# One recursion step of Strassen-Winograd: high and low matmuls in two series, and two weight sums made by accumulating transfers

## The chip, the core and the metric

The kernel runs on one core of a Trainium2 chip. A core has five engines with queues of their own: TensorE (PE; its weight loads are listed as PEld), VectorE (DVE), ScalarE (ACT), GpSimd (POOL) and SyncE (SP). SP, ACT and POOL also issue DMA transfers. The metric is the device time of one execution in microseconds (us), lower is better.

## The reference

One residual layer over 512 tokens of width 2048:

```
u = RMSNorm(h); [q|k|v|conv_a|conv_b|gate_attn|gate_conv] = u @ W_in
m = sigmoid(gate_attn) * y_attn + sigmoid(gate_conv) * y_conv
h = h + RMSNorm(m @ W_out)
h = h + RMSNorm((silu(u2 @ W_gate) * (u2 @ W_up)) @ W_down),   u2 = RMSNorm(h)
```

y_attn is a neighbourhood attention of 8 heads on an 8 x 64 grid with a learned bias, y_conv a gated depthwise convolution of width 31 with a layer norm. D_FF is 5632. All is float32.

## The kernel before, in words

Activations lie transposed: 16 tiles of 128 features by 512 tokens. Float32 products are made from rounded halves: x = high + low, and a product is high x high + high x low + low x high, three matmuls. A plain product (`gemm`) streams 512 columns per matmul and takes the weights in chunks of 512 KB: SP loads a chunk, ACT casts its high half (L124), DVE subtracts to get the low half (L125).

**The sigmoid gates and most of the feed-forward's first product go through `strassen` (L205).** One call makes two column blocks of 128 outputs for all 512 tokens. Its matrices are cut in two ways each: the inner dimension into features 0 to 1023 and 1024 to 2047, the tokens into halves A and B, and the outputs into two blocks, w0 and w1. So A11 and A12 are the halves of w0, A21 and A22 those of w1, and in Winograd's form seven products of quarter size do the work of eight:

```
S1 = A21 + A22, S2 = S1 - A11, S3 = A11 - A21, S4 = A12 - S2
T1 = B12 - B11, T2 = B22 - T1, T3 = B22 - B12, T4 = B21 - T2
A11 B11, A12 B21, S1 T1, S2 T2, S3 T3, S4 B22, A22 T4
```

(T4 and the place of A22 are such that the block of w1 comes out as p5 and y below.) The sums T are made once per stage by `winograd_t` (L190) and kept in SBUF, in slots whose first 256 columns are the high half and whose last 256 are the low half. The sums S are made in every call. `product` (L230) casts the weights' high half on ACT (L232), makes the low half on DVE (L234), and then, for each of 8 feature tiles, issues a matmul of the high weights with all 512 columns (L237: high and low activations at once) and one of the low weights with the first 256 columns (L238).

S1 is loaded by SP as A21 (L249), and GpSimd adds A22 to it in a transfer that accumulates (L250). S2, S3 and S4 are DVE sums (L222, L222, L266). A11, A21, A22 and A12 come by SP (`quarter`, L217), into six buffers that the stages of `gemm` use too. Three PSUM banks x, y and z take the products; ACT copies some out (`copied` L227, `done` L244), DVE adds (L257, L262, L264), and `joined` (L273) adds the two column halves of a result. There are 14 calls for the gates (L564, names g2 to g15) and 39 for the feed-forward (L740, names f5 to f43); between the two lie the rest of the mixer and the feed-forward's start.

**What sets the order.** The program is written in the order of the mathematics; a scheduler orders each engine's instructions by priority and by what is free, and places the buffers. A load is issued as soon as a buffer of its kind is free, and each DMA queue works in order. Only instructions handed to `keep_in_program_order` keep the order as written (some loads and the sums of squares). Activations, normalised inputs, T sums, results and squares share one pool `sp` of 66 slots of 2 KB per partition (L68). S1 has a kind of buffer of its own with two buffers of 4 KB ("S1"), the other sums another with two ("S"); at the end of the kernel loads of the residual use them as well (L798).

Of the kernel before, what the change touches and what calls it, by code (L numbers as in the profile page):

```python
# [25 lines left out]
F32 = mybir.dt.float32  # L26
F32R = mybir.dt.float32r
AF = mybir.ActivationFunctionType
ALU = mybir.AluOpType
AX = mybir.AxisListType  # L30

P = 128
# [30 lines left out]
def hybrid_block(ctx: ExitStack, tc, xT, vecs, rpb, mask, w_c0, w_qk, w_v, w_gg, w_cg, w_ao, w_co, w_out, w_g0, w_gu, w_dn, outT):  # L63
    nc = tc.nc
    PSUM = bass.MemoryType.PSUM
    const = ctx.enter_context(tc.tile_pool(name="const", bufs=1))
    wp = ctx.enter_context(tc.tile_pool(name="wp", bufs=3))
    sp = ctx.enter_context(tc.tile_pool(name="sp", bufs=66))  # L68
    sm_ctx = ExitStack()
    mm = ctx.enter_context(tc.tile_pool(name="mm", bufs=4, space=PSUM))  # L70
    at = ctx.enter_context(tc.tile_pool(name="at", bufs=4, space=PSUM))
# [4 lines left out]
    HT, HN = KT // 2, NT // 2  # L76
    A, B = slice(0, HN), slice(HN, NT)
# [4 lines left out]
    def bank(name):  # L82
        return mm.tile([P, NT], F32, tag="mm", name=name)
# [32 lines left out]
    def wchunk(src, name, parts=1):  # L116
        w = src.shape[-1]
        raw = wp.tile([P, 1024], F32, tag="raw", name=f"raw_{name}", bufs=6)[:, :w]
        hi = wp.tile([P, 1024], F32R, tag="whi", name=f"whi_{name}")[:, :w]
        lo = wp.tile([P, 1024], F32R, tag="wlo", name=f"wlo_{name}")[:, :w]  # L120
        for n in range(parts):
            s = slice(n * w // parts, (n + 1) * w // parts)
            nc.sync.dma_start(raw[:, s], src[:, s])
            nc.scalar.copy(hi[:, s], raw[:, s])  # L124
            nc.vector.tensor_tensor(out=lo[:, s], in0=raw[:, s], in1=hi[:, s].bitcast(F32), op=ALU.subtract)  # L125
        taps(rate)
        return hi, lo
# [61 lines left out]

    def winograd_t(u1, u2, t12, t34):  # L190

        nc.vector.tensor_tensor(out=t12[:, A], in0=u1[:, B], in1=u1[:, A], op=ALU.subtract)
        nc.vector.tensor_tensor(out=t12[:, B], in0=u2[:, B], in1=t12[:, A], op=ALU.subtract)
        nc.vector.tensor_tensor(out=t34[:, A], in0=u2[:, B], in1=u1[:, B], op=ALU.subtract)
        nc.vector.tensor_tensor(out=t34[:, B], in0=u2[:, A], in1=t12[:, B], op=ALU.subtract)

    def operands(b11, b2, t12, t34):
        return {
            "11": b11,
            **{n: [t[i] for t in b2] for i, n in enumerate(("21", "22"))},  # L200
            **{n: [t[i] for t in t12] for i, n in enumerate(("T1", "T2"))},
            **{n: [t[i] for t in t34] for i, n in enumerate(("T3", "T4"))},
        }

    def strassen(w0, w1, op, name, n):  # L205

        x, y, z = ((bank, abank)[n % 2](f"{name}_{i}") for i in range(3))

        def quarter(w, c):
            raw = wp.tile([P, 1024], F32, tag="raw", name=f"{name}q", bufs=6)
            nc.sync.dma_start(raw, w[:, c * 1024 : (c + 1) * 1024])  # L217
            return raw

        def wsum(a, b, op, i):  # L220
            t = stp.tile([P, 1024], F32, tag="S", name=f"{name}s{i}")
            nc.vector.tensor_tensor(out=t, in0=a, in1=b, op=op)  # L222
            return t

        def copied(ps, i):
            t = stp.tile([P, NT], F32, tag="quad", name=f"{name}v{i}", bufs=3)
            nc.scalar.copy(t, ps)  # L227
            return t

        def product(ps, w, b, first=False, last=False):  # L230
            hi = wp.tile([P, 1024], F32R, tag="whi", name=f"{name}h")
            nc.scalar.copy(hi, w)  # L232
            lo = wp.tile([P, 1024], F32R, tag="wlo", name=f"{name}l")
            nc.vector.tensor_tensor(out=lo, in0=w, in1=hi.bitcast(F32), op=ALU.subtract)  # L234
            for k, t in enumerate(op[b]):
                s = slice(k * P, (k + 1) * P)
                nc.tensor.matmul(ps, hi[:, s], t, start=first and k == 0, stop=False, skip_group_check=True)  # L237
                nc.tensor.matmul(  # L238
                    ps[:, A], lo[:, s], t[:, A], start=False, stop=last and k == HT - 1, skip_group_check=True
                )  # L240

        def done(ps, i):
            t = stp.tile([P, HN], F32, tag="half", name=f"{name}c{i}", bufs=2)
            nc.scalar.copy(t, ps[:, B])  # L244
            return ps[:, A], t


        s1 = stp.tile([P, 1024], F32, tag="S1", name=f"{name}s1")
        nc.sync.dma_start(s1, w1[:, :1024])  # L249
        nc.gpsimd.dma_start(s1, w1[:, 1024:], accum_op=ALU.add)  # L250
        a11, a21, a22, a12 = quarter(w0, 0), quarter(w1, 0), quarter(w1, 1), quarter(w0, 1)
        product(x, a11, "11", first=True)
        s2 = wsum(s1, a11, ALU.subtract, 2)
        p1 = copied(x, 1)
        product(y, s2, "T2", first=True)
        product(z, s1, "T1", first=True)
        nc.vector.tensor_tensor(out=y, in0=y, in1=p1, op=ALU.add)  # L257
        u2 = copied(y, 2)
        s3 = wsum(a11, a21, ALU.subtract, 3)
        product(y, s3, "T3")  # L260
        p5 = copied(z, 3)
        nc.vector.tensor_tensor(out=z, in0=z, in1=u2, op=ALU.add)  # L262
        product(x, a12, "21", last=True)
        nc.vector.tensor_tensor(out=p5, in0=y, in1=p5, op=ALU.add)  # L264
        s4 = s2
        nc.vector.tensor_tensor(out=s4, in0=a12, in1=s2, op=ALU.subtract)  # L266
        c11 = done(x, 1)
        product(z, s4, "22", last=True)
        c12 = done(z, 2)
        product(y, a22, "T4", last=True)  # L270
        return c11, c12, done(y, 3), (p5[:, A], p5[:, B])
# [117 lines left out]
    for c in range(HT):  # L389
# [3 lines left out]
        hi, lo = wchunk(w_c0[c], f"c0_{c}", 1 if c else 2)  # L393
# [33 lines left out]
    for half in range(2):  # L427
        rate = R_V[half]
        pv = [(bank, abank)[half](f"pv{half}_{t}") for t in range(NB)]
        for c in range(HT):  # L430
            if len(u) < 2 * c + 2:
                normalize(c)
            hi, lo = wchunk(w_v[half, :, c * 1024 : (c + 1) * 1024], f"v{half}_{c}")
            for k in range(2):
                s = slice(k * NT, (k + 1) * NT)
# [72 lines left out]
    for h in range(H):  # L508
        bm = bias_of(h)
        qk = []  # L510
        for i in range(2):
            ps = bank(f"qk{h}_{i}")
# [7 lines left out]
    stp = ctx.enter_context(tc.tile_pool(name="stp", bufs=2))  # L520
# [3 lines left out]
    b11, b2, t12, t34 = [], [], [], []  # L524
    pg = [bank(f"g0_{n}") for n in range(4)]
    for c in range(HT):
        hi, lo = wchunk(w_gg[c], f"g0_{c}")
        un = stp.tile([P, 2, NT], F32, tag="S", name=f"un{c}")
        for j, k in enumerate((c, c + HT)):
            ah, al = u[k]  # L530
            for n, ps in enumerate(pg):
                s = slice((j * 4 + n) * P, (j * 4 + n + 1) * P)
# [4 lines left out]
                out=un[:, j], in0=ah.bitcast(F32), in1=al.bitcast(F32), op=ALU.add  # L537
# [24 lines left out]
    op = operands(b11, b2, t12, t34)  # L562
    for i in range(2, KT):
        c11, c12, c21, c22 = strassen(w_cg[2 * CT + i], w_cg[2 * CT + KT + i], op, f"g{i}", i)  # L564
        if i == KT - 1:
            ya = [load_ya(h) for h in range(YA_EARLY)]
        ga, gb = slot(f"ga{i}"), slot(f"gb{i}")
        joined(ga[:, A], c11)
        joined(ga[:, B], c12)
        nc.scalar.activation(ga, ga, AF.Sigmoid)  # L570
        nc.scalar.dma_start(g_d[i], ga)
        joined(gb[:, B], c22)
        joined(gb[:, A], c21)
        nc.scalar.activation(gb, gb, AF.Sigmoid)
        nc.scalar.dma_start(g_d[KT + i], gb)


# [54 lines left out]
    f, acc = [], None  # L632
    for i in range(KT - 2):
        ps = bank(f"po{i}")
# [55 lines left out]
    for j in range(3):  # L690
        t = stp.tile([P, 2, NT], F32, tag="S", name=f"sg{j}")
        t, up = t[:, 0], t[:, 1]
# [10 lines left out]
    for c in range(HT):  # L703
        hi, lo = wchunk(w_g0[1, c], f"f1_{c}")
        for k in range(2):
            i = 2 * c + k
# [7 lines left out]
            for n in range(4):  # L714
                s = slice((k * 4 + n) * P, (k * 4 + n + 1) * P)
                for m, cols in enumerate((A, B)):
                    plain(pf[n][:, cols], hi[:, s], lo[:, s], moving[m], i + m == 0, i == KT - 1)
            if i >= HT:
                t12, t34 = slot(f"t12_{i}"), slot(f"t34_{i}")
# [3 lines left out]
    for j in range(2):  # L723
        t = slot(f"sg{3 + j}")
# [5 lines left out]
    op = operands(b11, b2, b_t12, b_t34)  # L730
# [6 lines left out]
    for j in range(5, FT):  # L737
        if j == FT - EARLY_AT:
            acts = [load(k) for k in range(EARLY)]
        c11, c12, c21, c22 = strassen(w_gu[j], w_gu[FT + j], op, f"f{j}", j)  # L740
        if j == FT - 1:
            acts += [load(k) for k in range(EARLY, EARLY + MORE)]
        t, up = slot(f"sg{j}"), slot(f"su{j}")
        joined(t[:, A], c11)
        joined(t[:, B], c12)
        nc.scalar.activation(t, t, AF.Silu)  # L746
        joined(up[:, B], c22)
        joined(up[:, A], c21)
        nc.vector.tensor_tensor(out=t, in0=t, in1=up, op=ALU.mult)
        nc.scalar.dma_start(a_d[j], t)  # L750


# [2 lines left out]
    for half in range(2):  # L755
        for g in range(KT // 2):
            last = half == 0 and g == KT // 2 - 1
# [37 lines left out]

    ha = []
    for i in range(0, KT - 4, 4):
        t = stp.tile([P, 4, HN], F32, tag="S" if i else "S1", name=f"ha{i}")  # L798
        nc.gpsimd.dma_start(t, h_d[i : i + 4, :, A].rearrange("k p t -> p k t"))
        ha += [t[:, m] for m in range(4)]  # L800
    for i in range(KT - 4, KT, 2):
        t = stp.tile([P, 2, HN], F32, tag="quad", name=f"ha{i}", bufs=3)
# [3 lines left out]
    s1, s2 = halves(r4, acc + sq, "r4", 0, pin=True)  # L806
# [107 lines left out]
```

## Time and profile before

| | us |
|---|---|
| median of 3 runs | 2596.47 (2594.53 to 2597.9) |
| the profiled execution's own time | 2599.95 |
| its span, first to last instruction | 2597.8 |
| TensorE busy | 2547.3 (98%) |
| VectorE busy | 1744.4 (67%) |
| ScalarE busy | 1074.8 (41%) |
| GpSimd busy | 264.7 (10%) |

The mean granted TensorE clock is 0.993 of full speed. 385.42 MB move by DMA, 148 GB/s over the span. Stages by the trace, from the span's start: convolution inputs, V and attention to 480 us; the sums T for the gates to 547; the gates' calls to 825; the output products of attention and convolution to 1005; W_out to 1190; the feed-forward's first chunk to 1263 and its sums T to 1312; its calls to 2085; the down projection to 2580; the last norm and the stores to 2598.

How to read it: the profile is one execution. Matmuls overlap, so the distance between the starts of two of them says what one costs, and not its own duration. In a timeline a row has its start in us, its duration in us, engine, line, operation, what it writes and reads, and behind it in brackets how long the engine had stood idle and what ended that.

### The profile page before, as it was taken

To read this page: it belongs to the slowest core of one execution; us is meant where nothing else is said; L and a number is where in the kernel's file an instruction comes from. 1 tells how busy PE (TensorE), PEld (TensorE's weight loads), DVE (VectorE), ACT (ScalarE), POOL (GpSimd) and SP (SyncE) were. 2 spreads that over 40 slices of the span, in tenths; PEclk is the share of its full clock that TensorE was granted. 3 is DMA by queue.
4 is the path that set the end of the run, shared out by engine and by line. 5 is a ranking of instruction groups with operands and counts; after the bars stand their busy time and mean duration, and the time that the engine had idled before them with its cause. 6 is when DMAs were issued, how large, how long until landed. Compare 5 with 4: busy or idle time off the path is not lost.

```text
span 2597.8 us, 33528 instructions
## 1 busy us (share of the span) xinstructions
PE 2547.3 (98%) x13078; PEld 2165.4 (83%) x13078; DVE 1744.4 (67%) x2224; ACT 1074.8 (41%) x1560; POOL 264.7 (10%) x290
## 2 busy tenths in 40 slices
PE   9999999999999999998999999999999999999996
PEld 8888888778888888887988888888888878888886
DVE  5999895677776654339887777777777842233336
ACT  5223333455555422224555555555555532233222
POOL 0110222320000021004100000000000110010003
PEclk9999999999999999999999999999999999999998
DMA  6244323356667445234356556555655653353334
GB/s 214 93 128 148 109 94 107 101 157 184 181 189 249 139 138 183 97 106 146 110 161 181 167 167 180 175 170 167 186 167 167 196 185 97 97 170 100 95 93 139
DMA packets 124623, 385.42 MB, mean 148 GB/s; under 512 B 14256, under 2 KB 21552, under 8 KB 124464
## 3 DMA queue, kind: packets, MB, share of 16 engines
q1 hardware_dynamic: 96464, 311.47, 36.8%
q0 software_dynamic: 13024, 45.62, 8.5%
q10 hardware_dynamic: 14976, 26.19, 2.7%
q8 instruction: 102, 1.67, 0.3%
q14 instruction: 57, 0.47, 0.1%
HBM read 350.72 MB, written 32.51 MB: 148 GB/s over the span
## 4 chain that ended last, share of the span: by engine, by line
PE 93%; DVE 4%; issue 1%; DMA 1%; ACT 1%; POOL 1%; POOLq 0%; DVEq 0%; ACTq 0%; SPq 0%
PE f L237 20%; PE f L238 10%; PE g L237 7%; PE pd L170 5%; PE pd L173 5%; PE pd L174 5%; PE g L238 4%; PE po L170 2%; PE po L173 2%; PE po L174 2%; PE qk L174 2%; PE qk L173 2%; PE qk L170 2%; PE py L174 2%; PE py L170 2%; PE py L173 2%
## 5 line engine op out<-in xcount | busy, mean ns | idle before, releaser
L125 DVE TENSOR_TENSOR wlo_wd<-raw_wd,whi_wd 128x1024 fp32r<-128x1024 f32 (+1 forms) x90 | 102.3, 1137 | 283.5 <-ACT whi_wd L124 283.5
L124 ACT CAST whi_wd<-raw_wd 128x1024 fp32r<-128x1024 f32 (+1 forms) x90 | 88.4, 982 | 311.8 <-PE pd L173 306.0
L375 DVE SCALAR_TENSOR_TENSOR cv<-z,vec,cv 128x497 f32<-128x497 f32 (+14 forms) x240 | 190.8, 797 | 4.7
L125 DVE TENSOR_TENSOR wlo_wo<-raw_wo,whi_wo 128x1024 fp32r<-128x1024 f32 x36 | 47.5, 1318 | 106.9 <-ACT whi_wo L124 106.9
L124 ACT CAST whi_wo<-raw_wo 128x1024 fp32r<-128x1024 f32 x36 | 37.9, 1054 | 130.0 <-PE po L173 122.6
L124 ACT CAST whi_qk<-raw_qk 128x1024 fp32r<-128x1024 f32 x32 | 33.6, 1051 | 77.1 <-PE qk L173 52.7
L124 ACT CAST whi_y<-raw_y 128x1024 fp32r<-128x1024 f32 x32 | 33.5, 1053 | 77.1 <-PE py L173 72.9
L125 DVE TENSOR_TENSOR wlo_qk<-raw_qk,whi_qk 128x1024 fp32r<-128x1024 f32 x32 | 40.4, 1261 | 32.3 <-ACT whi_qk L124 32.1
L125 DVE TENSOR_TENSOR wlo_y<-raw_y,whi_y 128x1024 fp32r<-128x1024 f32 x32 | 52.3, 1636 | 9.2 <-ACT whi_y L124 9.2
L615 DVE TENSOR_TENSOR gg<-py,gg 128x512 f32<-128x512 f32 x32 | 21.9, 690 | 51.7 <-PE py L174 51.4
L293 POOL TENSOR_TENSOR r_r<-r_v,mhalf 128x2 f32<-128x2 f32 (+1 forms) x6 | 7.7, 1284 | 458.3 <-DVE r_v L291 458.3
L734 POOL DMA_DIRECT2D ad<-a_d x44 | 24.1, 557 | 259.4 <-PE pd L170 196.5
L170 PE MATMUL py<-ycl,whi_y 128*128 128x512 f32 x128 | 49.8, 389 | 0.0
L173 PE MATMUL py<-ych,whi_y 128*128 128x512 f32 x128 | 49.8, 389 | 0.0
L174 PE MATMUL py<-ych,wlo_y 128*128 128x512 f32 x128 | 49.8, 389 | 0.0
L746 ACT ACTIVATE sg<-sg 128x512 f32<-128x512 f32 x39 | 24.7, 634 | 48.8 <-DVE sg L274 48.8
L454 POOL TENSOR_TENSOR bm<-braw,msk 128x128 f32<-128x128 f32 x56 | 43.2, 806 | 13.8 <-DMA braw<-in_rpb 13.8
L154 PE MATMUL f<-b,wlo_f 128*128 128x256 f32 x128 | 36.2, 283 | 0.0
L153 PE MATMUL f<-b,whi_f 128*128 128x256 f32 x128 | 36.2, 283 | 0.0
L152 PE MATMUL f<-b,whi_f 128*128 128x256 f32 x128 | 36.2, 283 | 0.0
L625 POOL TENSOR_TENSOR gg<-gg,gg 128x512 f32<-128x512 f32 x16 | 21.7, 1356 | 112.6 <-ACT whi_y L124 71.1
L124 ACT CAST whi_ca<-raw_ca 128x1024 fp32r<-128x1024 f32 x12 | 12.6, 1053 | 47.2 <-PE cb L173 19.0
(3045 smaller groups left out, 9196.8 us busy)
## 6 DMA issues: line engine op xcount, KB each, us to landing
raw_wd<-in_w_dn SPq DMA_DIRECT2D x60, 512.0 KB, 3.6
raw_wo<-in_w_out SPq DMA_DIRECT2D x36, 512.0 KB, 3.8
raw_qk<-in_w_qk SPq DMA_DIRECT2D x32, 512.0 KB, 3.8
raw_wd<-in_w_dn SPq DMA_DIRECT2D x30, 384.0 KB, 3.2
a_d<-sg ACTq DMA_DIRECT2D x44, 256.0 KB, 2.0
ad<-a_d POOLq DMA_DIRECT2D x44, 256.0 KB, 4.8
raw_v<-in_w_v SPq DMA_DIRECT2D x16, 512.0 KB, 4.3
raw_y<-in_w_ao SPq DMA_DIRECT2D x16, 512.0 KB, 3.6
```

Source lines behind the costliest of these rows:

```text
L124: nc.scalar.copy(hi[:, s], raw[:, s])
L125: nc.vector.tensor_tensor(out=lo[:, s], in0=raw[:, s], in1=hi[:, s].bitcast(F32), op=ALU.subtract)
L152: nc.tensor.matmul(o, hi, t[:, B], start=first, stop=False, skip_group_check=True)
L153: nc.tensor.matmul(o, hi, t[:, A], start=False, stop=False, skip_group_check=True)
L154: nc.tensor.matmul(o, lo, t[:, A], start=False, stop=last, skip_group_check=True)
L170: mmul = nc.tensor.matmul(ps, hi[:, s], al, start=first, stop=False)
L173: nc.tensor.matmul(ps, hi[:, s], ah, start=False, stop=False)
L174: nc.tensor.matmul(ps, lo[:, s], ah, start=False, stop=last)
L237: nc.tensor.matmul(ps, hi[:, s], t, start=first and k == 0, stop=False, skip_group_check=True)
L238: nc.tensor.matmul(ps[:, A], lo[:, s], t[:, A], start=False, stop=last and k == HT - 1, skip_group_check=True)
L375: nc.vector.scalar_tensor_tensor(out=a[:, to], in0=z[:, fr], scalar=col(C_WDW, i * CW + w), in1=a[:, to], op0=ALU.mult, op1=ALU.add)
L454: nc.gpsimd.tensor_tensor(out=bm[:, o + i - i0], in0=raw[:, :, i * BC : (i + 1) * BC], in1=msk[:, o + i - i0, None, :].broadcast_to([P, RO ...
```

## The change

The second block of outputs is computed with the opposite sign. With A21 and A22 taken as negated, S1 becomes -(A21 + A22), S2 becomes -(S1' + A11) with S1' = A21 + A22, S3 becomes A11 + A21 and S4 becomes A12 + S2'. So both S1' and S3 are sums of two quarters as they lie in memory, and each is now made by a plain load on SP and an accumulating load on GpSimd (`added`). The minus signs that are left go into T1, T2 and T4 (`winograd_t`, where two subtractions take the form -a - b in one scalar-tensor-tensor instruction), and the sign of the second block is turned back where it is used: a scale of -1 in the sigmoid of the second gate, and a factor of -1 in the multiply of the feed-forward. A21 alone is no longer loaded; A11 is loaded a second time as the ground of S3. S1' and S3 share a kind of buffer with three buffers ("SD"); to pay for the third, the pool of slots goes from 66 to 64. In `product` the eight matmuls with high weights now come first, and then the eight with low weights.

```diff
-    sp = ctx.enter_context(tc.tile_pool(name="sp", bufs=66))
+    sp = ctx.enter_context(tc.tile_pool(name="sp", bufs=64))
...
     def winograd_t(u1, u2, t12, t34):
-        nc.vector.tensor_tensor(out=t12[:, A], in0=u1[:, B], in1=u1[:, A], op=ALU.subtract)
-        nc.vector.tensor_tensor(out=t12[:, B], in0=u2[:, B], in1=t12[:, A], op=ALU.subtract)
+        def less(out, a, b):
+            nc.vector.scalar_tensor_tensor(out=out, in0=a, scalar=-1.0, in1=b, op0=ALU.mult, op1=ALU.subtract)
+        nc.vector.tensor_tensor(out=t12[:, A], in0=u1[:, A], in1=u1[:, B], op=ALU.subtract)
+        less(t12[:, B], t12[:, A], u2[:, B])
         nc.vector.tensor_tensor(out=t34[:, A], in0=u2[:, B], in1=u1[:, B], op=ALU.subtract)
-        nc.vector.tensor_tensor(out=t34[:, B], in0=u2[:, A], in1=t12[:, B], op=ALU.subtract)
+        less(t34[:, B], t12[:, B], u2[:, A])
...
-        def wsum(a, b, op, i):
-            t = stp.tile([P, 1024], F32, tag="S", name=f"{name}s{i}")
-            nc.vector.tensor_tensor(out=t, in0=a, in1=b, op=op)
+        def added(a, b, i):
+            t = stp.tile([P, 1024], F32, tag="SD", name=f"{name}s{i}", bufs=3)
+            nc.sync.dma_start(t, a)
+            nc.gpsimd.dma_start(t, b, accum_op=ALU.add)
             return t
...
+            ws = [slice(k * P, (k + 1) * P) for k in range(HT)]
             for k, t in enumerate(op[b]):
-                s = slice(k * P, (k + 1) * P)
-                nc.tensor.matmul(ps, hi[:, s], t, start=first and k == 0, stop=False, skip_group_check=True)
+                nc.tensor.matmul(ps, hi[:, ws[k]], t, start=first and k == 0, stop=False, skip_group_check=True)
+            for k, t in enumerate(op[b]):
                 nc.tensor.matmul(
-                    ps[:, A], lo[:, s], t[:, A], start=False, stop=last and k == HT - 1, skip_group_check=True
+                    ps[:, A], lo[:, ws[k]], t[:, A], start=False, stop=last and k == HT - 1, skip_group_check=True
                 )
...
-        s1 = stp.tile([P, 1024], F32, tag="S1", name=f"{name}s1")
-        nc.sync.dma_start(s1, w1[:, :1024])
-        nc.gpsimd.dma_start(s1, w1[:, 1024:], accum_op=ALU.add)
-        a11, a21, a22, a12 = quarter(w0, 0), quarter(w1, 0), quarter(w1, 1), quarter(w0, 1)
+        s1 = added(w1[:, :1024], w1[:, 1024:], 1)
+        a11 = quarter(w0, 0)
+        s3 = added(w0[:, :1024], w1[:, :1024], 3)
+        a12, a22 = quarter(w0, 1), quarter(w1, 1)
         product(x, a11, "11", first=True)
-        s2 = wsum(s1, a11, ALU.subtract, 2)
+        s2 = stp.tile([P, 1024], F32, tag="S", name=f"{name}s2")
+        nc.vector.tensor_tensor(out=s2, in0=s1, in1=a11, op=ALU.add)
...
-        s3 = wsum(a11, a21, ALU.subtract, 3)
...
-        nc.vector.tensor_tensor(out=s4, in0=a12, in1=s2, op=ALU.subtract)
+        nc.vector.tensor_tensor(out=s4, in0=a12, in1=s2, op=ALU.add)
...
-        nc.scalar.activation(gb, gb, AF.Sigmoid)
+        nc.scalar.activation(gb, gb, AF.Sigmoid, scale=-1.0)
...
-        nc.vector.tensor_tensor(out=t, in0=t, in1=up, op=ALU.mult)
+        nc.vector.scalar_tensor_tensor(out=t, in0=t, scalar=-1.0, in1=up, op0=ALU.mult, op1=ALU.mult)
...
-        t = stp.tile([P, 4, HN], F32, tag="S" if i else "S1", name=f"ha{i}")
+        t = stp.tile([P, 4, HN], F32, tag="S" if i else "SD", name=f"ha{i}", bufs=2 if i else 3)
```

## The prediction

> **What bounds the kernel now.** I read the page first (busy shares, the chain that ended last), then the windows by stage, then TensorE's timeline inside single stages. The page:
>
> ```profile
> span 2597.8 us, 33528 instructions
> PE 2547.3 (98%) x13078; PEld 2165.4 (83%) x13078; DVE 1744.4 (67%) x2224; ACT 1074.8 (41%) x1560; POOL 264.7 (10%) x290
> PE 93%; DVE 4%; issue 1%; DMA 1%; ACT 1%; POOL 1%; POOLq 0%; DVEq 0%; ACTq 0%; SPq 0%
> ```
>
> TensorE is busy for 98% of the span and holds 93% of the chain. The windows say in which stages that holds (columns: window, its length, then busy us and count of PE, PEld, DVE, ACT, POOL, then granted clock, DMA share, GB/s):
>
> ```profile
> 300.00:480.00 180.00, 179.81 (x872) 149.03 (x871) 134.96 (x241) 65.70 (x129) 46.77 (x62) 1.00 0.30 99
> 480.00:547.00 67.00, 57.87 (x250) 46.83 (x248) 53.56 (x102) 34.65 (x84) 31.34 (x35) 0.92 0.38 106
> 1190.00:1263.00 73.00, 64.91 (x306) 52.87 (x305) 66.67 (x82) 34.93 (x60) 31.18 (x17) 0.98 0.39 133
> 1263.00:1312.00 49.00, 49.00 (x400) 48.55 (x399) 46.65 (x102) 26.39 (x59) 3.40 (x1) 1.00 0.30 99
> 1312.00:1700.00 388.00, 388.00 (x2198) 336.40 (x2197) 305.75 (x352) 198.93 (x274) 17.57 (x20) 1.00 0.60 173
> ```
>
> In the last row, a stretch of `strassen` calls, TensorE never stops; VectorE is busy for 79% and the DMA engines for 60%. So work taken from VectorE there is worth nothing by itself, and only the time of the matmuls counts. TensorE does stop where the operands of `strassen` are prepared for the gates (480 to 547) and in the first chunk of the feed-forward (1190 to 1263). There are 14 + 39 = 53 calls (i = 2 to 15 for the gates, j = 5 to 43 for the feed-forward), each of 7 products of 8 pairs: a 512-column matmul with the high half of the weights (L237) and a 256-column one with the low half (L238). The length of a call, from the first starts of call 5 and of call 43:
>
> ```profile
> L238 PE MATMUL f<-t,f5l x32: 277/281/284, 1313.9 to 1330.5; 128*128 128x256 f32 x32
> L238 PE MATMUL f<-t,f43l x32: 277/281/284, 2065.8 to 2082.4; 128*128 128x256 f32 x32
> ```
>
> (2065.8 - 1313.9) / 38 = 19.787 us a call, with no stall that varies, hence 2.827 us a product and 353 ns a pair.
>
> **The order of the matmuls** is the part on which the sum rests. Today the pairs alternate; the change issues eight 512s and then eight 256s. The count of matmuls and of weight loads stays. What alternating costs is seen in the starts:
>
> ```profile
> 1353.59 0.40 PE L237 MATMUL f<-t,f7h 128*128 128x512 f32 x1
> 1353.83 0.28 PE L238 MATMUL f<-t,f7l 128*128 128x256 f32 x1
> 1353.95 0.40 PE L237 MATMUL f<-t,f7h 128*128 128x512 f32 x1
> ```
>
> 0.24 us from a 512 to the 256 after it, 0.12 back. Series of one size stand elsewhere in the trace: 512s straight behind the last `strassen` call, 512s behind a long run of 256s, and 256s behind 512s (first and last start; "..." stands for the equal rows between):
>
> ```profile
> 2082.52 0.40 PE L170 MATMUL pd<-fa0l,whi_wd 128*128 128x512 f32 x1
> ...
> 2084.36 0.39 PE L174 MATMUL pd<-fa2h,wlo_wd 128*128 128x512 f32 x1
> ...
> 2089.57 0.39 PE L173 MATMUL pd<-fa2h,whi_wd 128*128 128x512 f32 x1
> ```
>
> ```profile
> 1199.45 0.40 PE L185 MATMUL f<-u_4h,whi_f 128*128 128x512 f32 x1
> ...
> 1201.54 0.39 PE L185 MATMUL f<-u_4h,whi_f 128*128 128x512 f32 x1
> ```
>
> ```profile
> 1157.37 0.28 PE L170 MATMUL po<-m0l,whi_wo 128*128 128x256 f32 x1
> ...
> 1158.32 0.28 PE L174 MATMUL po<-m2h,wlo_wo 128*128 128x256 f32 x1
> ```
>
> Eight steps of 512 behind a 256 take 1.84 us (2082.52 to 2084.36); nine take 2.09 us in the second place, so eight take 1.86. Once such a series has run for a while it is quicker: the 23 steps from 2084.36 to 2089.57 take 226.5 ns each, eight of them 1.81 us. Eight steps of 256 take 0.95 us. So a product in the new order is 1.84 + 0.95 = 2.79 or 1.86 + 0.95 = 2.81, against 2.827. I take the middle, 2.80, since each new series of 512s begins behind a 256 and is too short (eight) to settle. That saves 27 ns a product; 53 x 7 = 371 products give **-9.9 us**. Bounds: 0 if alternating is not what costs the difference, and 2.827 - 1.81 - 0.95 = 65 ns a product, -24 us, if the whole series ran at the settled pace.
>
> The Trainium skill speaks against this term: "TensorE: Matmul & The Clock Gate", section "Back-to-back issue gap", gives a gap that depends on the column count alone, N / 2.4 + 2.5 ns when warm. By it a pair takes an estimated 109 + 216 = 325 ns in any order, and the term would be 0. The trace does not agree (353 ns for the pair in alternation, 226.5 for a settled 512), but it has no series of exactly eight and eight, so the rule stays as a rival.
>
> **The rest of the change, part by part.**
>
> VectorE loses one of its three sums per call (S3, L222) and keeps the others with another sign. Two subtractions of `winograd_t` become scalar-tensor-tensor instructions, as does the multiply at L749:
>
> ```profile
> 1579.52 1.22 DVE L222 TENSOR_TENSOR f19s<-f19q 128x1024 f32<-128x1024 f32 x1
> 538.27 0.41 DVE L193 TENSOR_TENSOR tt<-un,tt 128x256 f32<-128x256 f32 x1
> 1182.00 0.47 DVE L667 SCALAR_TENSOR_TENSOR u_0l<-f,vec,u_0h 128x256 fp32r<-128x256 f32 x1
> ```
>
> 53 x 1.22 = 65 us leave VectorE, all beside a TensorE that never waits for it in the calls: 0. The other form costs 0.06 us more for 256 columns: 2 x 8 of them are 1.0 us in the gates' preparation, where TensorE waits (57.87 of 67 us busy) and half may lie on the path, **+0.5**; the same 1.0 us in the feed-forward's preparation lies beside a full TensorE (49.00 of 49.00), and L749 comes behind its products with a whole call of time: 0. If that cover went, it would be 1 us, and twice 0.06 for each of 39 multiplies, 5 us. The sign inside the sigmoid is a factor of an activation that runs anyway: 0.
>
> At the first gate call the second product waited for its low half while only one high matmul had gone:
>
> ```profile
> 548.02 0.51 PE L237 MATMUL g<-t,g2h 128*128 128x512 f32 x1 [1.62 <-ACT g2h L232]
> 548.97 0.49 PE L237 MATMUL g<-t,g2h 128*128 128x512 f32 x1 [0.44 <-ACT g2h L232]
> ```
>
> With eight high matmuls first the 0.44 to 0.95 us go: **-0.7** (bounds 0 and -1).
>
> The queues: SP issues five plain loads per call before and after (the copy of A21 alone goes, a copy of A11 as the ground of S3 comes). GpSimd issues two accumulating loads instead of one, so 0.5 MB more per call. The rows for the one of today, from the page's queues, the tile of call 20's S1, line L250 and the timeline:
>
> ```profile
> q0 software_dynamic: 13024, 45.62, 8.5%
> L249 SPq DMA_DIRECT2D f20s<-in_w_gu x1: 327/327/327, 1571.3 to 1571.3; - x1
> L250 POOL DMA_DIRECT2D f20s<-in_w_gu x1: 876/876/876, 1575.7 to 1575.7; - x1
> L222 DVE TENSOR_TENSOR f20s<-f20s,f20q x1: 1215/1215/1215, 1594.3 to 1594.3; 128x1024 f32<-128x1024 f32 x1
> DMA to landing us min/median/max: 5.5/6.4/8.1
> 1571.57 1.05 ACT L232 CAST f18h<-f18s 128x1024 fp32r<-128x1024 f32 x1
> ```
>
> Queue 0, which has the accumulating loads, took 8.5% of 2597.8 us for 45.62 MB, so 2.5 us of all engines for 0.524 MB: the DMA share goes from 0.60 x 19.8 = 11.9 us to 14.4 of some 19.6, 74%. Is S3 in time? With three buffers for S1 and S3, S3 of the next call takes the one that S1 frees; that is today's moment of the plain load, 1571.3 in call 18. 4.4 us later GpSimd issues, and 6.4 us after that (the landing row of L250) it is there: 1582.1. Its cast to the high half stands at 1571.57 in call 18, so at 1591.4 in call 19: 9 us in hand. S1 now waits for S3's last reading instead, 2.5 us later (1573.9): it is there at about 1585, and its first reader came at 1594.3. GpSimd, 18 of 388 us busy, issues both in order; behind a waiting S1 or S3 on SP stand A12 and A22 of the same call, needed later still. Cost 0; if landing grew by more than 9 us, each us beyond costs up to 53.
>
> The pool of 2 KB slots goes from 66 to 64, and that pool is exhausted at one place at least, where the last two columns of W_out are done in halves:
>
> ```profile
> 1169.91 0.38 ACT L647 ACTIVATE f_sq<-po 128x256 f32<-128x256 f32 x1
> 1171.76 1.40 PE L284 MATMUL r_s<-ones,f_sq 128*128 128x1 f32 x12
> 1173.02 0.36 PE L170 MATMUL po<-m0l,whi_wo 128*128 128x256 f32 x1
> 1173.49 0.42 DVE L648 COPY f<-po 128x256 f32<-128x256 f32 x1
> ```
>
> Of what is alive there (32 slots of m, 16 of xr, 14 of f, the sum and two squares) little is left of 66: the copy of f15 at 1173.49 comes 3.6 us after its square, just behind the last reading of m0. With two slots less that square waits too, and the sum of squares (1171.76) can fall behind 24 matmuls, from 1173.02 to 1175.97: up to 2.9 us, in front of a stage where VectorE is busy 66.67 of 73 us. I take half: **+1.5** (bounds 0 and 2.9).
>
> **Sum**, against the profiled execution's own 2599.95 us (span 2597.8): -9.9 + 0.5 - 0.7 + 1.5 = -8.6, so 2591.3 us. The runs' median, 2596.47, lies 3.5 below that execution; on it the forecast is **2587.9 us**.
>
> **The rivals.**
>
> The order makes no difference to TensorE, by the page's rule or because the scheduler interleaves the products anyway. For it: a 256 in alternation takes 0.12 us like any other. Against it: the 512 takes 0.24 there. Then +1.3 remains: 2597.8.
>
> The series run settled: -24 + 1.3, so 2574. Against it: 2082.52 to 2084.36.
>
> Slower, by slots: with 64 the heads of the attention, which keep 32 slots of normalised input and 16 of V, find none for the transposed probabilities, and TensorE waits for one cast and one subtraction for each of 4 x 8 key blocks:
>
> ```profile
> 329.27 0.37 ACT L497 CAST pth<-pt 128x256 fp32r<-128x256 f32 x1 [0.23 <-PE pt L494]
> ```
>
> 0.37 + 0.41 (the two-operand row above) x 32 = 25 us; with -9.9 and the rest, 2613. Against it: TensorE was busy 179.81 of 180 us there, with later heads' products to fill in. It decides once half of the blocks wait, when it eats the gain.
>
> Slower, by late sums: two accumulating loads land over 9 us later than today; at 1 us beyond that, +53, so 2641. Against it: none landed in more than 8.1.
>
> **How the numbers follow.** Forecast 0.48, no difference 0.22, settled 0.12, slots 0.11, late sums 0.07. What a measurement can tell from no change is 0.2%, 5.2 us: faster is below 2591.3, slower above 2601.7. Faster: 0.12 and 0.45 of the forecast's 0.48, as a loss of slots up to 2.9 us or a gain nearer 6 can bring it inside: 0.57. Same: 0.03 + 0.22 and 0.03 of the mild cases of slots: 0.28. Slower: 0.15. The range goes from the settled case, 2573, to just above no difference, 2601; slots and late sums are left out.
>
> **What would show it.** In the profile after, a call of 19.6 us (19.4 if settled, 19.8 if the order is nothing); starts of L237's successor at 0.23 and of the low ones at 0.12; no VectorE row for S3 and two GpSimd rows per call; DMA share near 0.74 with TensorE still without waits from 1312 on; the sum of squares before the feed-forward up to 2.9 us later. I am wrong if the call is not shorter, or if TensorE shows new waits in the attention or for S1 or S3.

## The result, and the profile after

The changed kernel takes **2873.07 us** (median of 4 runs, 2870.77 to 2874.91), the kernel before 2596.57 beside it: ratio **1.1061**, 95% interval 1.1044 to 1.1077. The forecast was 2587.9 with a range up to 2601. It is wrong in size and in sign.

The page after, span and busy shares:

```profile
span 2869.0 us, 33750 instructions
PE 2638.8 (92%) x13078; PEld 2244.7 (78%) x13078; DVE 1681.7 (59%) x2171; ACT 1079.3 (38%) x1560; POOL 310.4 (11%) x343
```

TensorE has the same 13078 matmuls, but its share falls from 98% to 92%, and its busy time grows by 91 us all the same: it both stands and runs slower. Where? The windows by stage after (columns as in the prediction), a stretch of feed-forward calls:

```profile
1400.00:1700.00 300.00, 253.05 (x1308) 218.77 (x1307) 171.85 (x204) 120.67 (x166) 20.96 (x24) 0.90 0.60 157
```

In 300 us stand 1308 matmuls; TensorE is busy for 253 and its granted clock is 0.90. Before, it was busy without a break there at 1.00. The length of a call, from the first starts of calls 5 and 43 (the rows of both tiles after: shortest, median and longest duration in ns, then the first and the last start):

```profile
L247 PE MATMUL f<-b,f5h x24: 389/391/398, 1373.8 to 1389.4; 128*128 128x512 f32 x24
L247 PE MATMUL f<-b,f43h x24: 389/391/397, 2334.1 to 2349.6; 128*128 128x512 f32 x24
```

(2334.1 - 1373.8) / 38 = 25.27 us a call, against 19.79 before: 5.5 us more, and 5.5 x 53 is 290 us, a little over the loss of 276.5, since not every call grows. So the whole loss lies in the calls. What TensorE waits for there, from the list of its waits after (us in total, times, longest):

```profile
PE f L247 <- DVE f32v L274: 5.6, 1, 5.6
...
PE g L247 <- DVE g4v L274: 4.5, 1, 4.5
...
PE f L247 <- DVE f7v L274: 1.7, 1, 1.7
```

The list has such a wait, of 1.7 to 5.6 us, in 47 of the 53 calls, in the gates as in the feed-forward, and always for the same VectorE instruction: the add at L274, which must read the bank y before the last product (A22 T4) is added to it. The 47 rows (first and last shown) sum to 175 us. The add itself takes 0.69 us. The timeline of call 16 after shows what it stands behind:

```profile
1652.05 1.23 DVE L244 TENSOR_TENSOR f16l<-f16s,f16h 128x1024 fp32r<-128x1024 f32 x1 [0.48 <-ACT f16h L242]
1653.31 0.33 SPq L231 DMA_DIRECT2D f18s<-in_w_gu  x1
...
1657.30 2.00 PE L247 MATMUL f<-t,f16h 128*128 128x512 f32 x8
...
1658.44 0.87 POOL L232 DMA_DIRECT2D f18s<-in_w_gu  x1 [2.50 <-DMA f18s<-in_w_gu]
1658.82 0.69 DVE L272 TENSOR_TENSOR f<-f,f16v 128x512 f32<-128x512 f32 x1
1659.14 1.11 PE L249 MATMUL f<-t,f16l 128*128 128x256 f32 x8
...
1667.49 1.23 DVE L264 TENSOR_TENSOR f18s<-f18s,f18q 128x1024 f32<-128x1024 f32 x1 [7.97 <-issue]
1668.63 0.69 DVE L274 TENSOR_TENSOR f16v<-f,f16v 128x512 f32<-128x512 f32 x1
...
1669.46 3.54 PE L247 MATMUL f<-t,f16h 128*128 128x512 f32 x8 [3.62 <-DVE f16v L274]
1672.79 1.27 PE L249 MATMUL f<-t,f16l 128*128 128x256 f32 x8
...
1678.81 0.33 SPq L231 DMA_DIRECT2D f19s<-in_w_gu  x1
```

VectorE is done with the add L272 at 1659.5, and its next instruction is S2 (L264) of call **18**, two calls ahead of the one that is running. Its S1 isn't there: GpSimd issued the accumulating load at 1658.44, 1.1 us before VectorE was free, and S2 starts 9.05 us after the issue. The profile names no releaser ("issue"), but the landing row of the accumulating loads (line L232, from issue to landing) holds such a time:

```profile
DMA to landing us min/median/max: 6.4/8.6/10.6
```

VectorE stands for 7.97 us, and everything of call 16 stands behind it: L274, and so TensorE for 3.62 us. And it is a circle: S1 of call 18 could be loaded only when VectorE had read a buffer of its kind for the last time (1652.05 + 1.23 = 1653.28; SP issues at 1653.31), and the next such load, for call 19, is issued at 1678.81, after the VectorE work that S2 held up. From load to S2 14.2 us, from S2 to the next load 11.3: together 25.5, about the length of a call.

The matmuls behind the wait are slower: the series of eight 512s that begins at 1669.46 takes 3.33 us until the first 256 (1672.79); the one at 1657.30 took 1.84 (until 1659.14).

### The profile page after: what moved, and what is told of

Its sections match the earlier page's. It is cut to its first block, busy times and chain, and to the rows that moved or that the text cites. A ratio compares the mean times of both kernels' runs of the same rounds, so it can differ in the third digit from the quotient of the medians.

```text
span 2869.0 us, 33750 instructions
## 1 busy us (share of the span) xinstructions
PE 2638.8 (92%) x13078; PEld 2244.7 (78%) x13078; DVE 1681.7 (59%) x2171; ACT 1079.3 (38%) x1560; POOL 310.4 (11%) x343
## 5 line engine op out<-in xcount | busy, mean ns | idle before, releaser
L580 ACT ACTIVATE ga<-ga 128x512 f32<-128x512 f32 x14 | 8.8, 632 | 91.7 <-DVE ga L284 63.0
```

## The experiments

**Theory A**, formed on this trace: the change takes S3 off VectorE and out of the two "S" buffers, which in the calls then belong to S2 alone. With one of them free a call earlier, the scheduler puts S2 of call n + 2 into VectorE's order during call n, in front of work that TensorE waits for; its S1 has not landed. **Rival B**: two accumulating loads per call are late as such, wherever S2 stands. **Rival C**: the new order of the matmuls needs the operands in another rhythm. VectorE's order during call 17 supports A, but shows no time (behind the line of an add stands what it writes: the banks y and z or the sum p5; L234 and L244 make low halves):

```
before    L257 y  S2(18)  L234  L234  L262 z  S3(18)  L264 p5
after     L268 y          L244  L244  L272 z  S2(19)  L274 p5
```

### The new order of the matmuls alone (e1_order)

The kernel before, with nothing but the two series in `product`:

```diff
+            for k, t in enumerate(op[b]):
+                nc.tensor.matmul(ps, hi[:, ws[k]], t, ...)
             for k, t in enumerate(op[b]):
-                nc.tensor.matmul(ps, hi[:, s], t, ...)
                 nc.tensor.matmul(ps[:, A], lo[:, ws[k]], t[:, A], ...)
```

> The kernel before with the new order of matmuls alone (eight high, then eight low); sums, signs, buffers and slots as before. Theory A (the loss comes from S2: with two buffers of kind S for S2 alone, its VectorE sum is queued a call earlier than before, stands in front of work that TensorE needs, and waits there for S1's accumulating load): a call of 19.6 us, 2587 us (2583 to 2591), no waits in the calls. Rival B (the two accumulating loads of a call are late whatever stands in VectorE's queue): also 2587. Rival C (the series of matmuls, which want all low weights at once, make the loss): 2800 or more.

Measured: 2589.02 us, ratio 0.9968 (0.9958 to 0.9979). The windows and the tiles of calls 5 and 43 with the order alone:

```profile
1400.00:1700.00 300.00, 300.00 (x1719) 263.98 (x1718) 242.03 (x278) 156.57 (x215) 13.10 (x15) 1.00 0.62 178
```

```profile
L237 PE MATMUL f<-b,f5h x24: 389/391/398, 1309.7 to 1325.3; 128*128 128x512 f32 x24
L237 PE MATMUL f<-b,f43h x24: 389/391/398, 2052.7 to 2068.3; 128*128 128x512 f32 x24
```

TensorE is busy throughout, and a call lasts (2052.7 - 1309.7) / 38 = 19.55 us, 2.793 a product. The order is no loss, so C isn't the sole cause; it gains about what the prediction said.

### The whole change, S2 kept in program order (e2_pin)

S2 is handed to `keep_in_program_order`, "pinned" below: it then stands behind the low half of A11 of its own call.

```diff
-        nc.vector.tensor_tensor(out=s2, in0=s1, in1=a11, op=ALU.add)
+        tc.keep_in_program_order(nc.vector.tensor_tensor(out=s2, in0=s1, in1=a11, op=ALU.add))
```

> The changed kernel with one thing more: the VectorE sum S2 keeps its place in the program, behind the low half of A11 of its own call. Transfers, buffers, signs, order of matmuls as changed. Theory A: the wait of about 8 us in front of S2 goes, a call takes 19.6 us, 2588 us (2582 to 2596). Rival B: still near 2873, since S1 still lands when it did and its readers wait in other places. Rival C: near 2873.

Measured: 2587.92 us, ratio 0.9967 (0.9954 to 0.9979). So **one instruction's place in VectorE's order is worth 285 us**. The windows, the rows of tile f18s, and VectorE's row of the add L272 in call 16, with S2 pinned:

```profile
1400.00:1700.00 300.00, 300.00 (x1719) 263.93 (x1719) 224.50 (x262) 157.29 (x217) 26.24 (x30) 1.00 0.76 203
```

```profile
L232 POOL DMA_DIRECT2D f18s<-in_w_gu x2: 873/873/873, 1532.7 to 1550.3; - x2
L264 DVE TENSOR_TENSOR f18s<-f18s,f18q x1: 1220/1220/1220, 1558.5 to 1558.5; 128x1024 f32<-128x1024 f32 x1
...
DMA to landing us min/median/max: 4.3/6.5/9.1
```

```profile
1532.75 0.69 DVE L272 TENSOR_TENSOR f<-f,f16v 128x512 f32<-128x512 f32 x1
```

The transfers are the same two per call, as slow as in the kernel after (the landing row of line L232 has 8.7 us in the median and at most 10.2, against 8.6 and 10.6), and the DMA share is even higher, 0.76. B falls: they don't need to be faster. The accumulating load of S1 is issued at 1532.7 and there by 1541.8 at the latest (the tile's row has its plain and its accumulating loads together, at most 9.1 us); S2 wants it at 1558.5, 16.7 us later. Behind L272 of call 16, where S2 of call 18 stands in the kernel after, VectorE is free at 1533.4, 0.7 us behind the issue: there S2 would have to stand up to 8.4 us, before anything feeds back. In the kernel after it stood 7.97.

### The change without the order of the matmuls (e3_pairs)

`product` as before, in alternating pairs; all else as after.

> The changed kernel with the old alternating order of matmuls. In this program S2 of the call after next is still queued a call early on VectorE, but two places later than in the changed kernel, behind the sum into p5 (the one that TensorE waited for) and the low half of A22. Theory A: VectorE still waits for S1 in front of S2, 5 to 8 us per call, but with less work of TensorE behind it: between 2610 and 2880 us, with the wait visible at S2. Rival B: 2880, as changed plus the 10 us that the order saves. Rival C: about 2600.

Measured: 2815.56 us, ratio 1.0843 (1.0822 to 1.0864). The timeline of call 16 and the tiles of calls 5 and 43:

```profile
1653.28 1.23 DVE L263 TENSOR_TENSOR f18s<-f18s,f18q 128x1024 f32<-128x1024 f32 x1 [7.88 <-DMA f18s<-in_w_gu]
...
1655.69 0.39 PE L248 MATMUL f<-b,f17l 128*128 128x256 f32 x1 [3.86 <-DVE f17l L244]
```

```profile
L247 PE MATMUL f<-b,f5h x24: 395/398/404, 1369.0 to 1385.6; 128*128 128x512 f32 x24
L247 PE MATMUL f<-b,f43h x24: 395/398/404, 2278.3 to 2294.9; 128*128 128x512 f32 x24
```

Here the profile names the transfer itself: VectorE stands 7.88 us for the landing of f18s. Without the new order the loss remains, with a call of (2278.3 - 1369.0) / 38 = 23.93 us. Here the scheduler queues S2 two instructions later, behind the add p5 and a low half, so that TensorE misses a low half of the next call's weights (f17l). The loss is 58 us smaller than after; as the order by itself gains (e1_order), I put that down to the other place of S2, which was not measured apart. C falls altogether.

### The free buffer alone (e4_free)

The kernel before, with one accumulating load, S3 still on VectorE and the old order of matmuls; but S3 gets a buffer of its own, so that the two "S" buffers hold S2 alone, as they do after. The slots pay for it, 64 as after:

```diff
-            t = stp.tile([P, 1024], F32, tag="S", name=f"{name}s{i}")
+            t = stp.tile([P, 1024], F32, tag="S" if i == 2 else "S3", name=f"{name}s{i}", bufs=2 if i == 2 else 1)
```

> The kernel before (one accumulating load per call, S3 summed by VectorE, alternating order) with S3 in a buffer of its own, so that S2 has both buffers of kind S to itself, as in the changed kernel; 64 slots pay for it. S2 of the call after next is then queued a call early here too. Theory A: VectorE waits in front of S2 here as well, though less, since S1 is loaded 2.5 us earlier and lands sooner: some 3 to 6 us of wait per call, and 2620 to 2800 us. Rival B: about 2597. Rival C: about 2597.

Measured: 2771.1 us, ratio 1.0672 (1.0651 to 1.0693). The timeline in call 17 and the tiles of calls 5 and 43:

```profile
1644.73 0.88 POOL L250 DMA_DIRECT2D f19s<-in_w_gu  x1 [23.03 <-DMA f19s<-in_w_gu]
...
1653.03 1.23 DVE L222 TENSOR_TENSOR f19s<-f19s,f19q 128x1024 f32<-128x1024 f32 x1 [4.31 <-DMA f19s<-in_w_gu]
...
1655.00 0.47 PE L237 MATMUL f<-t,f17h 128*128 128x512 f32 x1 [0.70 <-DVE f17v L264]
```

```profile
L237 PE MATMUL f<-b,f5h x24: 395/398/403, 1356.8 to 1373.5; 128*128 128x512 f32 x24
L237 PE MATMUL f<-b,f43h x24: 395/398/403, 2234.2 to 2250.8; 128*128 128x512 f32 x24
```

**Giving a buffer more to a kernel that works, and nothing else in its calls, makes it 174 us slower.** S2 of call 19 stands in call 17; it starts 8.3 us after GpSimd's issue, and VectorE has stood 4.31 us for the transfer. TensorE's own wait for the add is short in this call (0.70 us, and 0.57 for the low half behind it); the list of its waits has up to 3.2 us in other calls. A call lasts (2234.2 - 1356.8) / 38 = 23.09 us. The second accumulating load is not needed for the loss, nor for the late landing: the landing row of L250 is 6.4/8.8/9.7 here, with one such load per call, against 5.5/6.4/8.1 in the kernel before. This settles A against B: where S2 stands makes it.

### S1 without its second half (e5_no_add)

The kernel after, unpinned, with S2 where it is in the kernel after, but without GpSimd's addition to S1:

```diff
-            nc.gpsimd.dma_start(t, b, accum_op=ALU.add)
+            if both:
+                nc.gpsimd.dma_start(t, b, accum_op=ALU.add)
...
-        s1 = added(w1[:, :1024], w1[:, 1024:], 1)
+        s1 = added(w1[:, :1024], w1[:, 1024:], 1, both=False)
```

> The kernel after, with the accumulating load of S1 left out: S1 is A21 alone, so the output is that of other weights and the work of the engines stays as it is. VectorE keeps the order of the kernel after, with the S2 sum of call n + 2 queued right behind the add L272 of call n (line numbers here one higher). Theory A (S2 is queued too early, and VectorE stands for the landing of the accumulating load): the plain load of A21 landed by about 1658.4 in the call of the kernel after in which S2 ran at 1667.5, and the add L272 in front of S2 was done at 1659.5; so S2 finds its operand, VectorE doesn't stand, the calls last 19.6 us and the time is 2586 to 2592 us. Rival (S2 waits for A11 or for its "S" buffer, which come no sooner): VectorE stands as before, and 2850 to 2875 us.

Measured: 2589.5 us, ratio 0.9973 (0.9960 to 0.9985). The timeline of call 22 (line numbers one higher than after):

```profile
1644.44 0.33 SPq L231 DMA_DIRECT2D f24s<-in_w_gu  x1
...
1649.96 0.69 DVE L273 TENSOR_TENSOR f<-f,f22v 128x512 f32<-128x512 f32 x1
...
1650.56 1.22 DVE L265 TENSOR_TENSOR f24s<-f24s,f24q 128x1024 f32<-128x1024 f32 x1
...
1651.70 0.68 DVE L275 TENSOR_TENSOR f22v<-f,f22v 128x512 f32<-128x512 f32 x1
```

S2 of call 24 is still queued in call 22 between the two adds, and VectorE goes through without a stop: the load is issued at 1644.44 and used at 1650.56. So the early place costs nothing by itself; it costs because a plain load and, behind it, an accumulating load don't fit into the time it leaves. A11 and the "S" buffer, the other things S2 waits for, are not what was late.

### One buffer for S2 (e9_one)

The other way round: the change as it is, nothing pinned, but one "S" buffer, and 66 slots (which it pays for).

```diff
-    sp = ctx.enter_context(tc.tile_pool(name="sp", bufs=64))
+    sp = ctx.enter_context(tc.tile_pool(name="sp", bufs=66))
...
-        s2 = stp.tile([P, 1024], F32, tag="S", name=f"{name}s2")
+        s2 = stp.tile([P, 1024], F32, tag="S", name=f"{name}s2", bufs=1)
```

(The tiles tt and sg, and one load of the residual, move to "SD".)

> The kernel after with one "S" buffer in place of two, so that S2 of a call needs the buffer of the call before, and 66 slots, which that buffer pays for (the temporary tiles tt and sg and the second load of the residual go to the "SD" buffers). Nothing is pinned; VectorE then has S2 of call n + 1, not n + 2, at the same place of call n, between the adds L272 and L274. Theory A (the loss is that S2 is queued a call too early): its S1 landed some 19 us sooner than it is wanted, VectorE doesn't stand, a call lasts 19.6 us, and the time is 2588 us, within 3, with DMA share 0.76 in the calls. Rival (it is the place between L272 and L274, or the two accumulating loads, whichever call S2 is of): 2850 us or more. If one buffer is too few, so that S2 comes late for its own cast: some us in each of 53 calls, 2640 us or more, with TensorE waiting for the high half of S2.

Measured: 2590.61 us, beside 2600.59 for the kernel before: ratio 0.9965 (0.9951 to 0.9978). Windows and tile f18s:

```profile
1400.00:1700.00 300.00, 300.00 (x1720) 264.18 (x1719) 224.16 (x263) 156.10 (x214) 27.13 (x31) 1.00 0.75 203
```

```profile
L232 POOL DMA_DIRECT2D f18s<-in_w_gu x2: 873/874/876, 1537.1 to 1553.6; - x2
L264 DVE TENSOR_TENSOR f18s<-f18s,f18q x1: 1215/1215/1215, 1557.5 to 1557.5; 128x1024 f32<-128x1024 f32 x1
```

VectorE's order in call 17 is the one shown for the kernel after, with S2(18) in the place of S2(19). That is enough: 20.4 us lie between issue and use. Taking a buffer away gives the forecast's time.

### A third accumulating load (e7_third)

With S2 pinned, A22 is added to S1 once more, to see how much time the transfers have in hand.

```diff
         s1 = added(w1[:, :1024], w1[:, 1024:], 1)
+        nc.gpsimd.dma_start(s1, w1[:, 1024:], accum_op=ALU.add)
```

> The kernel after with the S2 sum kept in program order, and a third accumulating load in each call: A22 is added to S1 twice, so the output is that of other weights. Theory A (with S2 in its old place the transfers have time in hand): the second addition waits for the first to land, 6.5 us, within the 17 us by which S1 was early, and the DMA share goes from 0.76 to about 0.89 in the calls; TensorE shows no waits, and the time stays at 2588 us, within 4. Rival (two accumulating loads are already near what the queue can give, so that the loss of the kernel after is one of the transfers and the pinned order only just escapes it): 2640 us or more, with waits behind S2.

Measured: 2601.15 us, ratio 1.0013 (1.0004 to 1.0022), 13 us over the pinned kernel: neither number. Windows and waits with the third load:

```profile
1400.00:1700.00 300.00, 300.00 (x1719) 263.97 (x1718) 223.38 (x261) 157.11 (x215) 40.28 (x46) 1.00 0.88 229
```

```profile
PE g L247 <- ACT gs L565: 7.5, 1, 7.5
PE py L170 <- DVE ya3l L135: 5.5, 1, 5.5
PE f L247 <- ACT f42h L242: 4.5, 1, 4.5
```

With two loads and S2 pinned the first two waits are 5.5 and 1.8 us, and the third doesn't stand in the list. From 1400 to 1700 us A holds: at a DMA share of 0.88 TensorE is busy for 300 of 300 us. The loss stands at the ends of the two series of calls: at the start of the gates' calls, in the first product behind them (ya3l) and in the second last call of the feed-forward, 2.0 + 3.7 + 4.5 = 10 us of longer waits, and slower matmuls behind them: from call 5 to call 43 the kernel takes 7.9 us longer than with two loads (751.0 against 743.1, by the first starts), 4.5 of them that wait. "Within 4" failed, since it looked at the steady calls alone.

### The slots alone (e8_order64)

The order of e1 with 64 slots in place of 66, a change of one number.

> The kernel before with the new order of the matmuls and the pool of slots cut from 66 to 64, nothing else. By the prediction's term the slots cost 1.5 us (0 to 2.9) over the new order with 66 slots (2589.0), so 2590.5 us. By the traces of the changed kernels, in which the squares' sum in front of the feed-forward came no later, 2589 us, within 1. If the attention loses its slots, 2613 us.

Measured: 2589.59 us, ratio 0.9971 (0.9960 to 0.9981), against 2589.02 and 0.9968 with 66: 0.6 us, inside the intervals. The first two squares in front of the feed-forward, from ScalarE's timeline with 64 and then with 66:

```profile
1165.00 0.38 ACT L648 ACTIVATE f_sq<-po 128x256 f32<-128x256 f32 x1
1170.76 0.38 ACT L648 ACTIVATE f_sq<-po 128x256 f32<-128x256 f32 x1
```

```profile
1164.49 0.38 ACT L648 ACTIVATE f_sq<-po 128x256 f32<-128x256 f32 x1
1167.37 0.38 ACT L648 ACTIVATE f_sq<-po 128x256 f32<-128x256 f32 x1
```

The second square does come 2.9 us later (5.76 after the first, not 2.88), but the third starts 13.29 us after the first in both (1178.29 and 1177.78): the delay is taken up before it counts.

### Longer series (e6_zigzag)

With S2 pinned, every second product issues its low matmuls first, so that series of 16 arise.

```diff
+            turn[0] += 1
+            todo = high + low if turn[0] % 2 else low + high
+            for n, (o, half, cols, k) in enumerate(todo):
```

> The kernel after with the S2 sum kept in program order, and every second product issued with its low matmuls first, so that two products make a series of 16 high and one of 16 low matmuls. If the settled pace (226.5 ns for a 512) comes within a series of 16 and only the first ones behind a 256 are slower, a product costs 2.80 us less about half of the 30 ns by which it is over 8 x 226.5 + 8 x 120 = 2772 ns: 371 x 15 ns = 5.6 us less than with the sum kept in order alone (2587.9), so 2582 us. If each 512 of a short series costs the same 230 ns whatever stands in front, 2588 us.

Measured: 2589.95 us, ratio 0.9969 (0.9960 to 0.9979): no gain over the pinned kernel (2587.92). TensorE's timeline:

```profile
1643.47 2.00 PE L253 MATMUL f<-b,f22h 128*128 128x512 f32 x8
1645.32 1.98 PE L253 MATMUL f<-t,f22h 128*128 128x512 f32 x8
1647.13 2.08 PE L253 MATMUL f<-t,f22l 128*128 128x256 f32 x16
```

The first eight 512s take 1.85 us, the second eight 1.81 (the settled pace), so the mechanism is there, but saves 0.04 us in two products; by 53 x 7 products that is at most 7 us. By the first starts of tiles f5h and f43h a call lasts (2052.8 - 1311.3) / 38 = 19.51 us, 0.04 less than in e1_order, which makes 2 us in 53 calls and isn't told apart from nothing here. No kernel of these runs is faster than the pinned one beyond the intervals; it, the order alone and the single buffer all stand at a ratio of 0.997.

## Why the prediction was wrong

**The bound** was read rightly: only time of the matmuls counts in the calls. What followed too quickly was that work taken from VectorE "is worth nothing by itself": S3's 1.22 us were worth nothing, but S3 also held a buffer.

**The order of the matmuls**: right. 2.80 us a product was forecast and 2.793 measured (e1_order), between the 2.79 and 2.81 of its two series; the call went from 19.787 to 19.553, and the time by -8.3 us (interval -10.9 to -5.5), where -9.9 was forecast. By the calls alone it would be 53 x 0.234 = 12.4 us, so a little was lost outside them: in the two profiles the gates' calls begin 0.7 us later with the new order, and from the start of the last of them to the start of the first of the feed-forward it takes 1.1 us more. (The bound of 65 ns and -24 us should read 67 ns and -25 us.) The formula that the prediction took from the Trainium skill, "TensorE: Matmul & The Clock Gate", section "Back-to-back issue gap", by which the order makes no difference, does not describe these pairs: the same matmuls take 34 ns less a product. The section gives it for an isolated gap, and says that in a stream of weight loads and matmuls both set the spacing; the prediction left that out.

**S3 leaves VectorE, the other forms, the first gate call**: "0", "+0.5" and "-0.7" were not measured apart; the second of the two waits for g2h did go with the order (2.1 us in two waits before, 1.6 in one in e1_order). All that the change does beside the order comes, with S2 pinned, to 2587.92 against 2589.02: nothing that the intervals show.

**The queues: this is the step that failed.** "Cost 0" rested on "it is there at about 1585, and its first reader came at 1594.3". The first half was nearly right: the accumulating loads land 8.6 us after their issue in the median (at most 10.6), 2.2 us later than the 6.4 taken, and the DMA share in the calls is 0.76 with S2 pinned where 74% was worked out. The second half took the time of S2 in the profile before as a need of the kernel. It was a place in an order that the scheduler makes anew, and that two buffers had held: before, S2 and S3 of a call filled both "S" buffers, so S2 could not be queued more than one call ahead. The change removed that bound without a wait or a priority being touched, and S2 went from behind the first add of one call to behind the second add of the call before. In the profile before, for S2 of call 19, these are

```profile
1559.13 0.69 DVE L262 TENSOR_TENSOR f<-f,f17v 128x512 f32<-128x512 f32 x1
...
1574.53 1.22 DVE L222 TENSOR_TENSOR f19s<-f19s,f19q 128x1024 f32<-128x1024 f32 x1
```

S2 stands there at 1574.5, 18.5 us behind the issue of its accumulating load (tile f19s, L250 at 1556.0). The new place begins at 1559.8, 14.7 us sooner and 3.8 us behind that issue: too early even for the 6.4 us that the landing took before. The runs show both sides: the free buffer alone makes the loss (e4_free, +174 us), the pinned instruction (e2_pin) or the missing buffer (e9_one) undoes it, and without the late operand the place is harmless (e5_no_add). Why the scheduler prefers S2 there wasn't shown; that its own estimate has the accumulating load land sooner than the 8.6 us is only argued. Whether one more "SD" buffer, and with it perhaps an earlier load of S1, would also undo the loss, no run tried.

**The price** was wrong with it. "Each us beyond costs up to 53" took a late S1 to hold up S1's reader alone. What stands behind it in VectorE's order belongs to the call that is running, and the stop delays the low halves that free the buffers for the next S1: the circle of 25.5 us. Of the 5.7 us a call (25.27 - 19.55), 3.6 in call 16 are TensorE's wait and most of the rest slower matmuls; over all calls 175 us of the loss are waits for L274.

**The slots**: right in the mechanism, mis-sized: the square came 2.9 us late as described, and cost 0.6 us, not told apart from 0, where 1.5 was taken.

**The rivals.** "Late sums" (2641, 0.07) named the operand, but wanted it later than before; the operand came as before and was wanted earlier. Its condition, landing over 9 us later, never came true (2.2 us in the median). The sum itself, 2587.9, is what the kernel does once S2 stays in place: 2587.92. What the last part of the prediction said would show it wrong, TensorE with new waits for S1, is what the waits show, one step removed: the row names L274, an add with nothing to do with S1, and only VectorE's timeline names S2.

## What to carry to other kernels

A buffer count is also a bound on how far ahead a scheduler can queue an instruction: whoever frees a buffer must ask which instruction will move up, on which in-order engine, and what then stands behind it. The start of a reader in the old trace is no deadline that survives the change; look for what holds it there (a buffer, a pin, a predecessor), and keep it by a pin or by the count if an operand by accumulating transfer comes late. Where a wait names an instruction that is itself quick and ready, read the row in front of it on its own engine.

## What was unexpected of the hardware

**A stop of 3.6 us costs half as much again.** After it (call 16) eight 512s took 3.33 us instead of 1.84, 416 ns each against 230, and the eight 256s behind them 1.11 us by their starts instead of 0.95: 1.65 us on top. After the 3.81 us of call 15 it lasts longer: 3.55 us, then 1.71, and the next eight 512s still take 2.12. The granted clock over the stretch of calls was 0.90. The Trainium skill, "TensorE: Matmul & The Clock Gate", section "Why this matters for your kernels", says that gaps of more than about 3 us between bursts drop the clock to half. The rows agree with the half (416 to 444 ns a 512 against 230), but not with 3 us as a limit. One of the shorter stops, from TensorE's timeline of the kernel after:

```profile
666.02 3.59 PE L247 MATMUL g<-t,g6h 128*128 128x512 f32 x8 [2.68 <-DVE g6v L274]
669.41 1.21 PE L249 MATMUL g<-t,g6l 128*128 128x256 f32 x8
```

Behind a stop of 2.68 us eight 512s take 3.39 us (669.41 - 666.02), and behind the other stops from 2.38 to 2.99 us they take 2.40 to 3.48. Behind 1.72 us (call f7) they take 1.90; but behind the 3.08 us of call g3 only 1.93. What decides between these, the runs don't show.

**The transfers stood far more than was feared.** At a DMA share of 0.88, with three accumulating loads in each call of 19.6 us, TensorE had no wait from 1400 to 1700 us (e7_third); what suffered were the two ends of the series of calls.
